# FFN of a hybrid encoder block: first weight sum by an accumulating DMA, 64 pairs by seven for 50, transposes' banks emptied by ScalarE

## The chip, the cores and the metric

The kernel runs on one core of a Trainium2 chip. The time is device microseconds of one execution. A core has TensorE (PE), VectorE (DVE), ScalarE (ACT), GpSimd (POOL) and SyncE (SP), each with its own in-order queue; here SP's queue issues nearly all DMAs and POOL's issues none.

## The reference

One layer of an encoder block on x of 256 tokens x 2048 channels, float32: a norm, a projection, a Hyena branch and a gated-MLP branch, their gated merge and an output projection, and then the part that matters here, a dense SwiGLU FFN with 5632 hidden channels:

```python
h = _rmsnorm(x, norm_ffn_g[l])
gate, up = jnp.split(jnp.einsum('bsd,df->bsf', h, w_ffn_in[l]), 2, axis=-1)
x = x + jnp.einsum('bsf,fd->bsd', jax.nn.silu(gate) * up, w_ffn_out[l])
...
return _rmsnorm(x, norm_final_g)
```

## The kernel before

**Precision by splits.** Every float32 operand of a matmul is split into a high and a low half of type fp32r: ACT casts the high half, DVE subtracts to get the low one (`split_to`, L66). A block product is three matmuls of 512 columns (high x high, high x low, low x high), accumulated in a PSUM bank.

**Weights.** All weights come through one list, `net.halves`. An entry is a 128 x 1024 piece of a weight, which `feed` loads into a "raw" buffer by a DMA on SP's queue and splits, or a function that does something of its own. `take(i)` makes sure that all entries up to i and five more (in the FFN) have been put into the engines' queues. There are six raw buffers and six pairs of high and low buffers.

**The FFN.** The hidden channels go in two parts. Part 0 has 6 chunks of 512 gate and 512 up channels, part 1 has 5. A chunk is one `Quad` over 8 pairs of input blocks: two 128-row blocks of the weight, two column groups of 512 (gate and up), two token tiles of 128. After a part's chunks, two output quads multiply the hidden values H by 12 pairs (part 0) or 10 (part 1) of the output weight. A plain pair has 2 x 2 x 2 = 8 block products (`plain`). A pair "by seven" (`seven`) has 7, by a scheme of Strassen's kind: P1 to P7 and Q4, Q5 use sums of the pair's weights and sums of the activations. P1, Q5, P7 and P6 take the four "aux" banks; P2, N3, Q4 and E, to which plain pairs add, take the other four. `PLAN_IN` and `PLAN_OUT` say which pairs go by seven: three per chunk, and 5, 5, 4 and 3 in the output quads, 50 in all.

**Weight sums.** A pair by seven needs four weights r1 to r4. `quads` makes them as list entries: `one` loads r1 (512 KB), the right half of r4 and the left half of r3 (256 KB each) and lets DVE add r2 = r1 + r4's right half on both halves (128 x 1024, L114), then splits r1; `two` adds r3's right half (512 wide, L119) and splits r2; `three` adds r4's left half (512 wide, L123) and splits r3; the last entry splits r4.

**Activation sums.** When a chunk's last bank is done, DVE combines (`sums`, `finish`), ACT applies silu and DVE multiplies by `up` (L581, two instructions per chunk: this document calls them the multiplications that end a chunk). Four ticks later, that is, after the next chunk's first two pairs, `turn` transposes the result into two aux banks, and the sink `to_h` reads each bank: for a pair that goes by seven in the output quads ACT copies it to the tile "xf" (L590), ACT casts it to H, DVE subtracts H's low half from the bank (L69), and `forms` makes four sums with four 128-wide DVE instructions (L371 to L374) and splits them to HE. Then the second bank's sink follows in the same order. The next quad's P1, Q5, P7 and P6 need aux banks too. `to_x2` does the same for the FFN's input X2, ACT and DVE both reading the bank.

Of the kernel before, what the change touches and what calls it, by code (L numbers as in the profile page):

```python
# [9 lines left out]
F32 = mybir.dt.float32  # L10
F32R = mybir.dt.float32r
# [27 lines left out]
class Net:  # L39
    def __init__(self, nc, tc, a):  # L40
        self.nc, self.tc, self.a = nc, tc, a
        self.halves = []
        self.parts = {}
        self.split_at = 0
        self.ws2 = None
        self.todo = []
        self.raws = self.pairs_ = -1


# [50 lines left out]

    def quads(self, src, seven):


        nc, first, r = self.nc, len(self.halves), {}
        if not seven:
            return self.line(src, 2)

        def one():
            for n in (1, 4, 3, 2):
                r[n] = self.raw_tile()  # L110
            nc.sync.dma_start(out=r[1], in_=src[0])
            nc.sync.dma_start(out=r[4][:, 512:1024], in_=src[1][:, 512:1024])
            nc.sync.dma_start(out=r[3][:, 0:512], in_=src[1][:, 0:512])
            nc.vector.tensor_tensor(out=r[2].rearrange("p (c n) -> p c n", c=2), in0=r[1].rearrange("p (c n) -> p c n", c=2),  # L114
                                    in1=r[4][:, 512:1024].unsqueeze(1).to_broadcast([P, 2, 512]), op=ALU.add)
            return self.split(r[1], 1024)

        def two():
            nc.vector.tensor_tensor(out=r[3][:, 512:1024], in0=r[2][:, 0:512], in1=r[1][:, 512:1024], op=ALU.add)  # L119
            return self.split(r[2], 1024)  # L120

        def three():
            nc.vector.tensor_tensor(out=r[4][:, 0:512], in0=r[3][:, 0:512], in1=r[3][:, 512:1024], op=ALU.add)  # L123
            return self.split(r[3], 1024)
        for fn in (one, two, three, lambda: self.split(r[4], 512)):
            self.halves.append((fn, None, None))
        return first

# [131 lines left out]
class Quad:  # L260
# [31 lines left out]
    def form(self, slot, n):  # L292
        return self.extra[:, slot, 0, n, :], self.extra[:, slot, 1, n, :]

# [5 lines left out]
    def seven(self, at, j, slot):  # L300
        net = self.net
        w = net.take(at)
        self.mul("P1", w, 0, self.at(2 * j, 0))
        self.mul("N3", w, 512, self.form(slot, 1))
        w = net.take(at + 1)
        self.mul("Q5", w, 0, self.form(slot, 2))
        self.mul("P7", w, 512, self.form(slot, 0))
        net.tick()
        w = net.take(at + 2)
        self.mul("P2", w, 0, self.at(2 * j + 1, 0))  # L310
        self.mul("P6", w, 512, self.form(slot, 3))
        w = net.take(at + 3)
        self.mul("Q4", w, 0, self.at(2 * j + 1, 1))
        net.tick()

    def sums(self):

        nc, b = self.net.nc, self.bank
        t = self.t = self.fx.tile([P, 3, 512], F32, name="T")
        d = self.d = self.fx.tile([P, 2, 512], F32, name="D")  # L320
        nc.scalar.copy(out=t[:, 1, :], in_=b["P1"])
        nc.vector.tensor_tensor(out=t[:, 0, :], in0=b["P6"], in1=t[:, 1, :], op=ALU.add)
        nc.vector.tensor_tensor(out=t[:, 2, :], in0=b["P7"], in1=t[:, 0, :], op=ALU.add)
        nc.vector.tensor_tensor(out=d, in0=b["Q5"].unsqueeze(1).to_broadcast([P, 2, 512]), in1=t[:, 0:3:2, :], op=ALU.subtract)
# [35 lines left out]

def forms_tile(fx):

    x = fx.tile([P, 7, P], F32, name="xf")
    return x, (x[:, 0:4:3, :], x[:, 1:3, :])


def forms(net, x, extra, slot):

    nc = net.nc
    x11, x12, x22, x21 = (x[:, n, :] for n in range(4))  # L370
    nc.vector.tensor_tensor(out=x[:, 5, :], in0=x21, in1=x22, op=ALU.subtract)  # L371
    nc.vector.tensor_tensor(out=x[:, 6, :], in0=x[:, 5, :], in1=x11, op=ALU.subtract)
    nc.vector.tensor_tensor(out=x[:, 4, :], in0=x[:, 6, :], in1=x12, op=ALU.add)
    nc.vector.tensor_tensor(out=x21, in0=x11, in1=x21, op=ALU.subtract)  # L374
    net.split_to(extra[:, slot, 0], extra[:, slot, 1], x[:, 3:7, :])

# [15 lines left out]
def build(nc, tc, a):  # L392
# [28 lines left out]
    wo_first = [net.line(a["wout"][n], 8) for n in range(4)]  # L421
    def quads(src, pl):
        return [net.quads(src[j], slot is not None) for j, slot in pl]
    fi_first, fo_first = [], []
    for part in range(2):
        for c in range(CHUNKS[part]):
            fi_first.append(quads(a["wfi"][c + 6 * part], PLAN_IN))
        for n in range(2):
            fo_first.append(quads(a[f"wfo{part}"][n], PLAN_OUT[part][n]))

    with ExitStack() as top:
# [9 lines left out]
        const.tile([P, 40], F32, name="const_pad")  # L441
        ones = net.ones = const.tile([P, P], F32, name="ones")
        nc.vector.memset(ones, 1.0)
        ident = net.ident = const.tile([P, P], F32, name="ident")
# [48 lines left out]
        for n in range(4):  # L493
# [17 lines left out]
        for n in range(4):  # L511
# [4 lines left out]
            if n == 0:  # L516
# [3 lines left out]
                fx = sd.enter_context(tc.tile_pool(name="fx", bufs=1))  # L520
                x2s = ExitStack()
                x2pool = x2s.enter_context(tc.tile_pool(name="x2pool", bufs=1))
                X2 = x2pool.tile([P, KD, 512], F32R, name="X2")
                XE = x2pool.tile([P, 3, 2, 4, P], F32R, name="XE")
            else:
# [7 lines left out]

            def to_x2(n, c):
# [30 lines left out]
        for part in range(2):  # L565
            H = HE = None
            for c in range(CHUNKS[part]):
# [3 lines left out]
                if c == 0:  # L571
# [626 lines left out]
```

## Time and profile before

| | |
|---|---|
| median of three runs | 1366.54 us (1366.52 to 1371.71) |
| the profiled execution's own time | 1369.54 us |
| its span, first to last instruction | 1367.7 us |
| PE / DVE / ACT / POOL busy | 98% / 84% / 57% / 0% |
| mean granted clock of TensorE | 0.997 |
| DMA, mean over the span | 205 GB/s, 280.24 MB |

Busy shares are of the span. The FFN begins near 640 us and takes the rest. A matmul's duration in the trace includes its latency, and matmuls overlap, so the time from one start to the next is the one to count with.

### The profile page before, as it was taken

Reading aid. Unit: us, or ns where it says so; the run is one execution under the profiler, and the core shown is the slowest. Engines: PE = TensorE matmul, PEld = TensorE weight load, DVE = VectorE, ACT = ScalarE, POOL = GpSimd, SP = SyncE. Lnnn points to the kernel's source line nnn. Section 1 sums busy time; section 2 is a strip of 40 time slices with the busy share of each in tenths; the row PEclk is TensorE's granted clock in tenths of the full one; section 3 lists DMA queues with packets and bytes.
Section 4 is the critical chain, followed back from the end, with each engine's and each line's share of the span. In section 5 each row is a group of like instructions: output and inputs, shape, how many; then the busy total and the mean of one; then the engine's idle time right before and its main releaser. Section 6 shows DMA issues by size and latency. Waiting matters only on the chain.

```text
span 1367.7 us, 17785 instructions
## 1 busy us (share of the span) xinstructions
PE 1345.1 (98%) x6404; PEld 1124.0 (82%) x6404; DVE 1143.5 (84%) x1552; ACT 777.4 (57%) x1002; POOL 0.7 (0%) x6
## 2 busy tenths in 40 slices
PE   9999999999999999999999999999999999999996
PEld 7888888888888888888888877878888788878885
DVE  7887789798888766556898989989888889989996
ACT  7665555455545444455666665655555566666653
POOL 0000000000000000000000000000000000000000
PEclk9999999999999999999999999999999999999999
DMA  8775656556555696675556566566766566558853
GB/s 288 254 239 177 193 170 202 168 177 208 164 183 154 233 337 219 183 240 179 197 170 199 200 200 209 163 197 188 243 207 224 185 201 215 172 179 296 281 182 120
DMA packets 89961, 280.24 MB, mean 205 GB/s; under 512 B 9993, under 2 KB 10897, under 8 KB 89233
## 3 DMA queue, kind: packets, MB, share of 16 engines
q1 hardware_dynamic: 87424, 274.84, 61.9%
q10 hardware_dynamic: 2448, 4.27, 0.8%
q8 instruction: 50, 0.82, 0.2%
q14 instruction: 39, 0.31, 0.1%
HBM read 268.58 MB, written 10.49 MB: 204 GB/s over the span
## 4 chain that ended last, share of the span: by engine, by line
PE 83%; DVE 10%; DMA 4%; issue 3%; ACT 1%; DVEq 0%; SPq 0%; ACTq 0%
PE mm L283 16%; PE mg L283 13%; PE mm L138 9%; PE aux L283 8%; PE mg L172 6%; PE mg L174 6%; PE mg L173 6%; PE mm L140 4%; DVE wlo L69 4%; PE mm L174 2%; PE mm L173 2%; PE mm L172 2%; DMA raw<-in_wfi 2%; PE aux L787 2%; DVE raw L114 1%
## 5 line engine op out<-in xcount | busy, mean ns | idle before, releaser
L68 ACT CAST whi<-raw 128x1024 fp32r<-128x1024 f32 (+1 forms) x575 | 572.2, 1010 | 480.8 <-PE mm L283 84.5
L69 DVE TENSOR_TENSOR wlo<-raw,whi 128x1024 fp32r<-128x1024 f32 (+1 forms) x575 | 662.0, 1170 | 165.9 <-ACT whi L68 161.3
L283 PE MATMUL mm<-whi,X 128*128 128x512 f32 x506 | 179.5, 390 | 0.0
L283 PE MATMUL mg<-whi,X 128*128 128x512 f32 x506 | 174.0, 390 | 0.2 <-ACT ne L351 0.2
L138 PE MATMUL mm<-X,whi 128*128 128x512 f32 x512 | 161.4, 396 | 0.0
L140 PEld LDWEIGHTS mm<-X,wlo 128*128 128x128 f32 x512 | 96.1, 188 | 22.6
L283 PEld LDWEIGHTS mg<-whi,X 128*128 128x128 f32 x506 | 95.1, 188 | 20.7 <-ACT ne L351 0.7
L283 PEld LDWEIGHTS mm<-whi,X 128*128 128x128 f32 x506 | 95.3, 188 | 19.9
L140 PE MATMUL mm<-X,wlo 128*128 128x256 f32 x512 | 101.0, 278 | 0.0
L172 PE MATMUL mg<-whi,X 128*128 128x512 f32 x256 | 101.0, 394 | 0.0
L173 PE MATMUL mg<-wlo,X 128*128 128x512 f32 x256 | 99.9, 390 | 0.0
L174 PE MATMUL mg<-whi,X 128*128 128x512 f32 x256 | 99.8, 391 | 0.0
L283 PE MATMUL mm<-wlo,X 128*128 128x512 f32 x253 | 98.7, 390 | 0.0
L283 PE MATMUL mg<-wlo,X 128*128 128x512 f32 x253 | 98.5, 389 | 0.0
L283 PE MATMUL mm<-whi,H 128*128 128x512 f32 x250 | 87.9, 389 | 0.0
L283 PE MATMUL mg<-whi,H 128*128 128x512 f32 x250 | 85.4, 390 | 0.5 <-ACT ne L351 0.5
L283 PE MATMUL aux<-whi,XE 128*128 128x512 f32 x198 | 74.8, 398 | 7.0 <-DVE H L69 6.9
L138 PEld LDWEIGHTS mm<-X,whi 128*128 128x128 f32 x512 | 79.0, 189 | 1.1
L114 DVE TENSOR_TENSOR raw<-raw 128x1024 f32<-128x1024 f32 x50 | 61.0, 1221 | 21.8 <-DMA raw<-in_wfi 12.7
L174 PEld LDWEIGHTS mg<-whi,X 128*128 128x128 f32 x256 | 48.1, 188 | 10.2
L283 PEld LDWEIGHTS mm<-wlo,X 128*128 128x128 f32 x253 | 47.6, 188 | 9.9
L283 PEld LDWEIGHTS mg<-whi,H 128*128 128x128 f32 x250 | 46.9, 188 | 10.6 <-ACT ne L351 0.9
(285 smaller groups left out, 2228.0 us busy)
## 6 DMA issues: line engine op xcount, KB each, us to landing
raw<-in_wfi SPq DMA_DIRECT2D x143, 512.0 KB, 4.2
raw<-in_wfo SPq DMA_DIRECT2D x71, 512.0 KB, 4.3
raw<-in_wg SPq DMA_DIRECT2D x64, 512.0 KB, 3.6
raw<-in_win SPq DMA_DIRECT2D x64, 512.0 KB, 3.6
raw<-in_wfi SPq DMA_DIRECT2D x66, 256.0 KB, 3.1
raw<-in_wbr SPq DMA_DIRECT2D x32, 512.0 KB, 5.5
raw<-in_wout SPq DMA_DIRECT2D x32, 512.0 KB, 3.7
raw<-in_wfo SPq DMA_DIRECT2D x34, 256.0 KB, 3.4
```

Of the source, the lines that this page charges most:

```text
L68: self.nc.scalar.copy(out=hi, in_=src)
L69: self.nc.vector.tensor_tensor(out=lo, in0=src, in1=hi.bitcast(F32), op=ALU.subtract)
L114: nc.vector.tensor_tensor(out=r[2].rearrange("p (c n) -> p c n", c=2), in0=r[1].rearrange("p (c n) -> p c n", c=2), in1=r[4][:, 512:1024]. ...
L138: nc.tensor.matmul(ps[:, 0:512], lhsT=hi[:, col:col + P], rhs=mov, start=start, stop=False)
L140: nc.tensor.matmul(ps[:, 0:256], lhsT=lo[:, col:col + P], rhs=mov[:, 0:256], start=False, stop=stop)
L172: self.nc.tensor.matmul(ps[tt], lhsT=xh, rhs=wh, start=start, stop=False)
L173: self.nc.tensor.matmul(ps[tt], lhsT=xh, rhs=wl, start=False, stop=False)
L174: self.nc.tensor.matmul(ps[tt], lhsT=xl, rhs=wh, start=False, stop=stop)
L283: self.net.nc.tensor.matmul(ps, lhsT=l, rhs=r, start=(n == 0), stop=(n == self.total[name] - 1))
L787: nc.tensor.matmul(ps[:, ri, :], lhsT=fw[:, m + ri, :], rhs=z, start=(n == 0), stop=(n == 2))
```

## The change

Three things are changed, with some moves of memory to make room.

1. r2 is made by DMA. A new list entry, `early`, stands in front of the pair before: SP loads the pair's first piece into a new tile "racc" (two buffers, 512 KB), and POOL issues a DMA that adds the right half of the second piece, read twice from DRAM, onto both halves of it (`accum_op=ALU.add`). `one` then loads r1 (the first piece once more) and r3's left half, without r4's right half; `two` takes "racc" as r2.
2. `PLAN_IN` has four pairs by seven per chunk (2, 3, 5, 6) for three (2, 4, 6); the last two output quads have five each for four and three, the last of them in another order of pairs.
3. In `to_h` ACT copies the bank to SBUF (into "pq", whose content has been transposed) and casts the high half from there; DVE's low half and `forms` follow three or four ticks later. `to_x2` likewise has ACT copy the bank with the scale, and splits from SBUF. `forms` stores three of its sums in the extra tile and the fourth in the place of a block that pairs by seven do not use.

The tile "t5" has four buffers for six, "D" is part of "T", and "ones" lies in another pool.

```diff
+    def quads(self, src, pl):
+        nc, firsts = self.nc, []
+        def early(src):
+            def fn():
+                r2 = self.racc = self.rpool.tile([P, 1024], F32, name="racc", bufs=2)
+                nc.sync.dma_start(out=r2, in_=src[0])
+                nc.gpsimd.dma_start(out=r2.rearrange("p (c n) -> p c n", c=2),
+                                    in_=src[1][:, 512:1024].unsqueeze(1).to_broadcast([P, 2, 512]), accum_op=ALU.add)
+                self.raccs.append(r2)
+            return fn
+        def pieces(src):
+            r = {}
+            def one():
+                for n in (1, 4, 3):
+                    r[n] = self.raw_tile()
+                nc.sync.dma_start(out=r[1], in_=src[0])
+                nc.sync.dma_start(out=r[3][:, 0:512], in_=src[1][:, 0:512])
+                return self.split(r[1], 1024)
+            def two():
+                r[2] = self.raccs.pop(0)
+                nc.vector.tensor_tensor(out=r[3][:, 512:1024], in0=r[2][:, 0:512], in1=r[1][:, 512:1024], op=ALU.add)
+                return self.split(r[2], 1024)
+            def three():
+                nc.vector.tensor_tensor(out=r[4][:, 0:512], in0=r[3][:, 0:512], in1=r[3][:, 512:1024], op=ALU.add)
+                return self.split(r[3], 1024)
+            return one, two, three, lambda: self.split(r[4], 512)
+        for n, (j, slot) in enumerate(pl):
+            if n + 1 < len(pl) and pl[n + 1][1] is not None:
+                self.halves.append((early(src[pl[n + 1][0]]), None, None))
+            firsts.append(len(self.halves))
+            if slot is None:
+                self.line(src[j], 2)
+            else:
+                for fn in pieces(src[j]):
+                    self.halves.append((fn, None, None))
+        return firsts
...
     def form(self, slot, n):
-        return self.extra[:, slot, 0, n, :], self.extra[:, slot, 1, n, :]
+        m = (1, 3, 0, 2)[n]
+        if m == 3:
+            return self.at(2 * slot[1], 1)
+        return self.extra[:, slot[0], 0, m, :], self.extra[:, slot[0], 1, m, :]
...
-        t = self.t = self.fx.tile([P, 3, 512], F32, name="T")
-        d = self.d = self.fx.tile([P, 2, 512], F32, name="D")
+        t = self.t = self.fx.tile([P, 4, 512], F32, name="T")
+        d = self.d = t[:, 0:4:3, :]
...
+def forms(net, fx, x, extra, slot, mov, j):
 
     nc = net.nc
-    x11, x12, x22, x21 = (x[:, n, :] for n in range(4))
-    nc.vector.tensor_tensor(out=x[:, 5, :], in0=x21, in1=x22, op=ALU.subtract)
-    nc.vector.tensor_tensor(out=x[:, 6, :], in0=x[:, 5, :], in1=x11, op=ALU.subtract)
-    nc.vector.tensor_tensor(out=x[:, 4, :], in0=x[:, 6, :], in1=x12, op=ALU.add)
-    nc.vector.tensor_tensor(out=x21, in0=x11, in1=x21, op=ALU.subtract)
-    net.split_to(extra[:, slot, 0], extra[:, slot, 1], x[:, 3:7, :])
+    f = fx.tile([P, 4, P], F32, name="xf")
+    x11, x21, x12, x22 = (x[:, b, P * t:P * (t + 1)] for b in range(2) for t in range(2))
+    nc.vector.tensor_tensor(out=f[:, 0, :], in0=x21, in1=x22, op=ALU.subtract)
+    nc.vector.tensor_tensor(out=f[:, 1, :], in0=x11, in1=x21, op=ALU.subtract)
+    nc.vector.tensor_tensor(out=f[:, 2, :], in0=f[:, 0, :], in1=x11, op=ALU.subtract)
+    nc.vector.tensor_tensor(out=f[:, 3, :], in0=f[:, 2, :], in1=x12, op=ALU.add)
+    net.split_to(extra[:, slot, 0], extra[:, slot, 1], f[:, 0:3, :])
+    net.split_to(mov[:, 2 * j, P:L], mov[:, 2 * j, L + P:2 * L], f[:, 3, :])
...
-PLAN_IN = plan(range(8), (2, 4, 6))
-PLAN_OUT = [[plan(range(12), (2, 4, 6, 8, 10))] * 2, [plan(range(10), (2, 4, 6, 8)), plan(range(10), (2, 4, 6))]]
+PLAN_IN = plan(range(8), (2, 3, 5, 6))
+PLAN_OUT = [[plan(range(12), (2, 4, 6, 8, 10))] * 2,
+            [plan(p, (2, 4, 5, 7, 8)) for p in (range(10), (0, 2, 1, 4, 5, 3, 7, 8, 6, 9))]]
...
-                    t = mpool.tile([P, 512], F32, name="t5", bufs=6)
+                    t = mpool.tile([P, 512], F32, name="t5", bufs=4)
...
+            def to_x2(n, c, xn=xn):
                 def sink(pt):
                     slot = dict(PLAN_IN)[2 * n + c]
+                    flat = xn[:, c, :].rearrange("p (b t) -> p b t", b=2)
+                    j = 4 * n + 2 * c
+                    for b in range(2):
+                        nc.scalar.activation(out=flat[:, b, :], in_=pt[:, b, :], func=AF.Identity,
+                                             scale=par[:, PC_GFFN + j + b:PC_GFFN + j + b + 1])
+                    net.split_to(X2[:, j:j + 2, 0:L], X2[:, j:j + 2, L:2 * L], flat)
                     if slot is not None:
-                        x, halves = forms_tile(fx)
-                        for b in range(2):
-                            j = 4 * n + 2 * c + b
-                            nc.scalar.activation(out=halves[b], in_=pt[:, b, :].rearrange("p (t i) -> p t i", t=2),
-                                                 func=AF.Identity, scale=par[:, PC_GFFN + j:PC_GFFN + j + 1])
-                    for b in range(2):
-                        j = 4 * n + 2 * c + b
-                        gcol = par[:, PC_GFFN + j:PC_GFFN + j + 1]
-                        nc.scalar.activation(out=X2[:, j, 0:L], in_=pt[:, b, :], func=AF.Identity, scale=gcol)
-                        nc.vector.scalar_tensor_tensor(out=X2[:, j, L:2 * L], in0=pt[:, b, :], scalar=gcol,
-                                                       in1=X2[:, j, 0:L].bitcast(F32), op0=ALU.mult, op1=ALU.subtract)
-                    if slot is not None:
-                        forms(net, x, XE, slot)
+                        forms(net, fx, flat, XE, slot, X2, 2 * n + c)
...
-                def to_h(j, H=H, HE=HE, slots=dict(PLAN_OUT[part][0])):
+                def to_h(j, pq=pq, H=H, HE=HE, slots=dict(PLAN_OUT[part][0])):
                     def sink(pt):
                         slot = slots[j]
-                        if slot is not None:
-                            x, halves = forms_tile(fx)
-                            for b in range(2):
-                                nc.scalar.copy(out=halves[b], in_=pt[:, b, :].rearrange("p (t i) -> p t i", t=2))
-                        net.split_to(H[:, 2 * j:2 * j + 2, 0:L], H[:, 2 * j:2 * j + 2, L:2 * L], pt)
-                        if slot is not None:
-                            forms(net, x, HE, slot)
+                        flat = pq[:, j % 2, :].rearrange("p (b t) -> p b t", b=2)
+                        nc.scalar.copy(out=flat, in_=pt)
+                        hi, lo = H[:, 2 * j:2 * j + 2, 0:L], H[:, 2 * j:2 * j + 2, L:2 * L]
+                        nc.scalar.copy(out=hi, in_=flat)
+                        def rest():
+                            nc.vector.tensor_tensor(out=lo, in0=flat, in1=hi.bitcast(F32), op=ALU.subtract)
+                            if slot is not None:
+                                forms(net, fx, flat, HE, slot, H, j)
+                        net.later(3 + j % 2, rest)
```

The lines of the old `quads` and `forms` that go are in the listing above.

## Rows read from the trace of the kernel before

**Rows 1.** The page: span, busy time of each engine, the large DMA queue.

```profile
span 1367.7 us, 17785 instructions
...
PE 1345.1 (98%) x6404; PEld 1124.0 (82%) x6404; DVE 1143.5 (84%) x1552; ACT 777.4 (57%) x1002; POOL 0.7 (0%) x6
...
q1 hardware_dynamic: 87424, 274.84, 61.9%
```

**Rows 2.** Windows: length; PE, PEld, DVE, ACT, POOL busy (instructions); granted clock; DMA share; GB/s.

```profile
783.30:827.50 44.20, 43.05 (x195) 35.25 (x194) 39.70 (x46) 26.84 (x34) 0.00 (x0) 1.00 0.57 190
827.50:871.70 44.20, 42.64 (x192) 35.10 (x191) 41.29 (x48) 27.17 (x34) 0.00 (x0) 1.00 0.62 202
1080.00:1100.00 20.00, 17.75 (x76) 14.26 (x75) 18.03 (x21) 10.51 (x14) 0.00 (x0) 0.91 0.48 147
1240.00:1260.00 20.00, 20.00 (x90) 16.57 (x89) 18.27 (x20) 12.63 (x17) 0.00 (x0) 1.00 0.79 289
1260.00:1280.00 20.00, 20.00 (x93) 16.36 (x92) 20.00 (x23) 11.32 (x15) 0.00 (x0) 1.00 0.86 322
```

**Rows 3.** Waits of TensorE, 700 to 1300 us: total, times, longest.

```profile
PE aux L283 <- DVE H L69: 8.4, 5, 2.3
```

**Rows 4.** Timeline of a bank wait: start, length (us), engine, line, operation, count.

```profile
826.19 0.33 SPq L111 DMA_DIRECT2D raw<-in_wfi  x1
...
830.45 1.03 PE L203 MATMUL aux<-ident,pq 128*128 128x128 f32 x8
...
831.24 0.48 PE L283 MATMUL aux<-whi,X 128*128 128x512 f32 x1
...
831.71 0.64 ACT L590 COPY xf<-aux 128x256 f32<-128x256 f32 x2
...
832.03 1.22 DVE L114 TENSOR_TENSOR raw<-raw 128x1024 f32<-128x1024 f32 x1
...
835.03 0.68 DVE L69 TENSOR_TENSOR H<-aux,H 128x512 fp32r<-128x512 f32 x1
835.63 0.28 DVE L371 TENSOR_TENSOR xf<-xf 128x128 f32<-128x128 f32 x1
...
835.77 0.50 PE L283 MATMUL aux<-whi,XE 128*128 128x512 f32 x1 [1.56 <-DVE H L69]
835.83 0.69 DVE L69 TENSOR_TENSOR H<-aux,H 128x512 fp32r<-128x512 f32 x1
...
837.03 2.35 DVE L69 TENSOR_TENSOR wlo<-raw,whi 128x1024 fp32r<-128x1024 f32 x2
```

**Rows 5.** Chain that ended last: start, length, what.

```profile
727.20 2.04 PE mg L283 x9
```

**Rows 6.** Groups by shape, 700 to 1300 us: count, busy, mean ns, idle before.

```profile
L114 DVE TENSOR_TENSOR raw<-raw 128x1024 f32<-128x1024 f32 x43 | 52.5, 1221 | 18.9 <-DMA raw<-in_wfi 9.8 <-DMA raw<-in_wfo 9.1
...
L68 ACT CAST whi<-raw 128x512 fp32r<-128x512 f32 x43 | 26.7, 620 | 35.0 <-DVE raw L123 35.0
...
L68 ACT CAST H<-aux 128x512 fp32r<-128x512 f32 x22 | 11.9, 600 | 0.0
```

**Rows 7.** Timeline of VectorE: the multiplications that end a chunk.

```profile
696.52 1.42 DVE L581 SCALAR_TENSOR_TENSOR pq<-ne,r,pq 128x512 f32<-128x512 f32 x2
...
826.04 1.41 DVE L581 SCALAR_TENSOR_TENSOR pq<-ne,r,pq 128x512 f32<-128x512 f32 x2
...
913.92 1.42 DVE L581 SCALAR_TENSOR_TENSOR pq<-ne,r,pq 128x512 f32<-128x512 f32 x2
```

**Rows 8.** DMA issues: KB each, median us to landing; landings of tile raw.

```profile
raw<-in_wfi SPq DMA_DIRECT2D x143, 512.0 KB, 4.2
yacc<-y_d SPq DMA_DIRECT2D x2, 1024.0 KB, 10.8
other<-p_d SPq DMA_DIRECT2D x2, 1024.0 KB, 8.9
DMA to landing us min/median/max: 2.6/3.9/8.1
```

More of the change, by code (lines that the diff above doesn't have):

```diff
@@ L47, in __init__ @@
         self.raws = self.pairs_ = -1
+        self.raccs = []
     def chunk(self, pieces, cuts=1):
@@ L99, in feed @@
             self.split_at += 1
[L101 to L127, printed above, removed]
@@ L303, in seven @@
         self.mul("P1", w, 0, self.at(2 * j, 0))
-        self.mul("N3", w, 512, self.form(slot, 1))
+        self.mul("N3", w, 512, self.form((slot, j), 1))
         w = net.take(at + 1)
-        self.mul("Q5", w, 0, self.form(slot, 2))
-        self.mul("P7", w, 512, self.form(slot, 0))
+        self.mul("Q5", w, 0, self.form((slot, j), 2))
+        self.mul("P7", w, 512, self.form((slot, j), 0))
         net.tick()
@@ L310, in seven @@
         self.mul("P2", w, 0, self.at(2 * j + 1, 0))
-        self.mul("P6", w, 512, self.form(slot, 3))
+        self.mul("P6", w, 512, self.form((slot, j), 3))
         w = net.take(at + 3)
@@ L358, in finish @@
         nc.vector.tensor_tensor(out=ne, in0=ne, in1=self.d, op=ALU.add)
[L361 to L367, printed above, removed]
+def forms(net, fx, x, extra, slot, mov, j):
     nc = net.nc
-    x11, x12, x22, x21 = (x[:, n, :] for n in range(4))
-    nc.vector.tensor_tensor(out=x[:, 5, :], in0=x21, in1=x22, op=ALU.subtract)
-    nc.vector.tensor_tensor(out=x[:, 6, :], in0=x[:, 5, :], in1=x11, op=ALU.subtract)
-    nc.vector.tensor_tensor(out=x[:, 4, :], in0=x[:, 6, :], in1=x12, op=ALU.add)
-    nc.vector.tensor_tensor(out=x21, in0=x11, in1=x21, op=ALU.subtract)
-    net.split_to(extra[:, slot, 0], extra[:, slot, 1], x[:, 3:7, :])
+    f = fx.tile([P, 4, P], F32, name="xf")
[6 more added lines that the diff above has]
+    net.split_to(mov[:, 2 * j, P:L], mov[:, 2 * j, L + P:2 * L], f[:, 3, :])
 def plan(pairs, seven):
     return [(j, seven.index(j) if j in seven else None) for j in pairs]
-PLAN_IN = plan(range(8), (2, 4, 6))
-PLAN_OUT = [[plan(range(12), (2, 4, 6, 8, 10))] * 2, [plan(range(10), (2, 4, 6, 8)), plan(range(10), (2, 4, 6))]]
+PLAN_IN = plan(range(8), (2, 3, 5, 6))
+PLAN_OUT = [[plan(range(12), (2, 4, 6, 8, 10))] * 2,
+            [plan(p, (2, 4, 5, 7, 8)) for p in (range(10), (0, 2, 1, 4, 5, 3, 7, 8, 6, 9))]]
 CHUNKS = (6, 5)
@@ L421, in build @@
     wo_first = [net.line(a["wout"][n], 8) for n in range(4)]
-    def quads(src, pl):
-        return [net.quads(src[j], slot is not None) for j, slot in pl]
     fi_first, fo_first = [], []
@@ L426, in build @@
         for c in range(CHUNKS[part]):
-            fi_first.append(quads(a["wfi"][c + 6 * part], PLAN_IN))
+            fi_first.append(net.quads(a["wfi"][c + 6 * part], PLAN_IN))
         for n in range(2):
-            fo_first.append(quads(a[f"wfo{part}"][n], PLAN_OUT[part][n]))
+            fo_first.append(net.quads(a[f"wfo{part}"][n], PLAN_OUT[part][n]))
     with ExitStack() as top:
@@ L441, in build @@
         const.tile([P, 40], F32, name="const_pad")
-        ones = net.ones = const.tile([P, P], F32, name="ones")
-        nc.vector.memset(ones, 1.0)
         ident = net.ident = const.tile([P, P], F32, name="ident")
@@ L453, in build @@
         ev = left.enter_context(tc.tile_pool(name="ev", bufs=1))
+        ones = net.ones = ev.tile([P, P], F32, name="ones")
+        nc.vector.memset(ones, 1.0)
         ys_pool = left.enter_context(tc.tile_pool(name="ys_pool", bufs=1))
@@ L521, in build @@
                 x2s = ExitStack()
+                net.rpool = sd.enter_context(tc.tile_pool(name="rpool", bufs=1))
                 x2pool = x2s.enter_context(tc.tile_pool(name="x2pool", bufs=1))
                 X2 = x2pool.tile([P, KD, 512], F32R, name="X2")
-                XE = x2pool.tile([P, 3, 2, 4, P], F32R, name="XE")
+                XE = x2pool.tile([P, 4, 2, 3, P], F32R, name="XE")
             else:
@@ L532, in build @@
                 nc.scalar.activation(out=sq[:, 0, :], in_=y, func=AF.Square, accum_out=ss[:, 0, tt, n:n + 1])
-            def to_x2(n, c):
+            xn = fx.tile([P, 2, 512], F32, name="ne")
+            def to_x2(n, c, xn=xn):
                 def sink(pt):
                     slot = dict(PLAN_IN)[2 * n + c]
-                    if slot is not None:
-                        x, halves = forms_tile(fx)
-                        for b in range(2):
-                            j = 4 * n + 2 * c + b
-                            nc.scalar.activation(out=halves[b], in_=pt[:, b, :].rearrange("p (t i) -> p t i", t=2),
-                                                 func=AF.Identity, scale=par[:, PC_GFFN + j:PC_GFFN + j + 1])
-                    for b in range(2):
-                        j = 4 * n + 2 * c + b
-                        gcol = par[:, PC_GFFN + j:PC_GFFN + j + 1]
-                        nc.scalar.activation(out=X2[:, j, 0:L], in_=pt[:, b, :], func=AF.Identity, scale=gcol)
-                        nc.vector.scalar_tensor_tensor(out=X2[:, j, L:2 * L], in0=pt[:, b, :], scalar=gcol,
-                                                       in1=X2[:, j, 0:L].bitcast(F32), op0=ALU.mult, op1=ALU.subtract)
-                    if slot is not None:
-                        forms(net, x, XE, slot)
+                    flat = xn[:, c, :].rearrange("p (b t) -> p b t", b=2)
[4 more added lines that the diff above has]
+                    net.split_to(X2[:, j:j + 2, 0:L], X2[:, j:j + 2, L:2 * L], flat)
+                    if slot is not None:
+                        forms(net, fx, flat, XE, slot, X2, 2 * n + c)
                 return sink
@@ L576, in build @@
                     H = hpool.tile([P, 24, 512], F32R, name="H")
-                    HE = hpool.tile([P, 5, 2, 4, P], F32R, name="HE")
+                    HE = hpool.tile([P, 5, 2, 3, P], F32R, name="HE")
                 q.finish(pq, ne)
```

## The prediction

> **What bounds the kernel now.** I read the page's busy shares first. TensorE (PE) is busy for 1345.1 of 1367.7 us, VectorE (DVE) for 84%, ScalarE (ACT) for 57%, POOL for 0.7 us in all; the one large DMA queue fills 61.9% of the engines' time [rows 1]. So at most 22.6 us can come from filling PE's gaps, and anything beyond that must take matmuls away. Next, windows over the FFN, since all that the change touches lies behind 600 us. In two windows of 44.2 us, about one chunk each, PE is idle 1.2 and 1.6 us, DVE busy 39.7 and 41.3 us, the DMA engines 57 and 62% [rows 2]. PE bounds, with DVE close behind. The table of PE's waits between 700 and 1300 us names one cause: 8.4 us, in five waits, for DVE's low half of H [rows 3]. The timeline of one of them shows how [rows 4]. Eight transposes run at 830.45; ACT copies the `forms` operands out of the first bank at 831.71, but DVE has a weight sum and two more instructions ahead of its own read of that bank and reaches it at 835.03, and the second bank at 835.83. PE, which needs these banks for P7 and P6 of the first pair by seven, sits idle 1.56 us before 835.77. Around one such wait the granted clock is 0.91 over 20 us [rows 2], so 1.8 us go there beside the wait.
>
> **Matmuls removed.** A plain pair is 8 block products of 3 matmuls, a pair by seven 7 of 3. In the chain of waits nine matmuls in a row take 2.04 us [rows 5]: 0.227 us each. (The 0.48 and 0.50 us of single ones in [rows 4] are latency, not pitch.) Fourteen more pairs by seven (one in each of 11 chunks, three in the last two output quads) remove 14 x 3 x 0.227 = 9.5 us. They lie where PE is the bound, so all of it counts.
>
> **The banks' emptying.** After the change ACT alone reads them: copy, high half, copy, high half, some 0.6 us each by the H cast of [rows 6], 2.4 us for both banks, the low halves and `forms` coming three or four ticks later from SBUF. P7 follows the transposes by 9 matmuls, 2.0 us, and P6 by 2.7 or more; the first bank is free after 0.6 us, the second after 1.8. What can hold ACT is the cast of the pair's fourth weight, queued in front, which needs DVE's two short sums. Placed on the times of that chunk: the multiplications at a chunk's end run from 826.04 to 827.45 [rows 7]; DVE then needs 1.13 + 0.60 + 1.13 + 0.60 us up to that sum, to 830.9; the cast ends at 831.5, after the transposes (831.24), and the banks are free at 832.1 and 833.3. P7 wants its bank at 831.24 + 2.04 = 833.3, P6 at 834.0: it fits, by about a microsecond. So the 8.4 us and the 1.8 us of clock go: 10.2 us. A check: multiplications lie (913.92 - 696.52) / 5 = 43.5 us apart [rows 7], while 183 matmuls x 0.227 and 0.8 us of transposes [rows 4] make 42.3 us: 1.2 us are lost per chunk, about ten times.
>
> **DVE.** Two 1024-wide instructions in a row take 2.35 us, so 1.13 each, a 512-wide one is followed after 0.60 us, a 128-wide one after 0.20 [rows 4]. A chunk before: 5 plain pairs x 2 x 1.13 = 11.3; 3 by seven x (4 x 1.13 + 3 x 0.60) = 19.0; sums, `finish` and multiplications 0.6 + 0.6 + 3 x 1.13 + 1.4 = 6.0; H 2 x 0.6 and, for nine chunks in ten, `forms` 4 x 0.2 + 0.6: 2.5. Together 38.8 us. After: 4 x 2.26 = 9.0; 4 x (3 x 1.13 + 3 x 0.60) = 20.8; 6.0; 2.6: 38.4 us, against 180 x 0.227 + 0.8 = 41.6 us on PE. The first sum, 50 x 1.22 us (L114, of which [rows 6] has 43), more than pays for the added pairs. DVE stays under PE with 3 us to spare per chunk, and its 18.9 us of waits for DMA before L114 [rows 6] go. ACT gets 1.5 casts more per added pair and a copy per bank, some 2.5 us on the 27 of [rows 2]; DVE is the later of the two in any case, so this is hidden unless ACT blocks. Dropping "t5" to four buffers and moving "ones" costs nothing: a fourth-back "t5" has been read by its add or transposes several ticks earlier.
>
> **The accumulating DMA.** Its chain per pair: SP's issue, 0.33 us; the load of "racc", 512 KB, median 4.2 us [rows 8]; POOL's issue; the accumulation; then DVE's second sum and ACT's cast. No row shows the last DMA. POOL's issue lies between SP's 0.33 us [rows 4] and 5.5 us, the spread of landings between 2.6 and 8.1 [rows 8]; I take 0.33. The accumulation brings 512 KB and has to read the 512 KB that are there: it is nearest to the 1024 KB rows, 8.9 and 10.8 us [rows 8]; below, a fast plain load, 2.6; above, two slow ones, 16.2. I take 8.9. Sum 13.8 us, ends 5.9 and 30 (0.33 + 2.6 + 0.33 + 2.6; 0.33 + 8.1 + 5.5 + 16.2).
>
> The time it has: two "racc" buffers, so the load for pair 5 waits for pair 2's second split, that for 6 for pair 3's. From there to the second sum of 5 DVE does, with 1.73 for a short sum and a long split, 1.73 + 0.6 (rest of 2), 1.13 + 1.73 + 1.73 + 0.6 (pair 3), 2.26 (pair 4), 2.6 (H, `forms`) and 1.13 (first split of 5) = 13.5 us, paced by PE some 14.6; the second sum itself may come about 2 us late before PE starves, since splits run several halves ahead. So up to 16.5 us nothing is lost. In the output quads a pair by seven follows a plain one, or the buffer is free earlier, and 14.5 to 17 us are there. SP's queue is held while it waits for "racc", with the r1 and r3 loads of the next pair behind; r1 of pair 5 then lands some 6 us after pair 3's second split, and DVE wants it after 7.
>
> Bandwidth: a chunk moved 8 x 1.05 = 8.4 MB (190 and 202 GB/s [rows 2]). After, a pair by seven moves 0.52 + 0.52 + 0.26 + 0.52 = 1.83 MB, 2.36 with the read of the tile: 11.5 to 13.6 MB in 41.6 us, 277 to 328 GB/s. The stretch at 322 GB/s had the engines at 0.86 [rows 2], which makes 374 the ceiling. It fits, but not everywhere: between 1240 and 1280 us, where `yacc` and `other` come in, (289 + 322) x 20 us = 12.2 MB move [rows 2]; four pairs by seven there add 3.1 to 5.2 MB, against 15.0 MB of room: 0.3 to 2.4 MB too much, 1 to 6 us, of which I take 3. For the thinner cover elsewhere I take 0.25 us for each of ten chunks, 2.5.
>
> **Sum.** The profiled execution took 1369.54 us, 1.84 more than its span and 3.0 above the median of the runs. 1369.5 - 9.5 - 10.2 + 5.5 = 1355.3; less 3.0, 1352.
>
> **Rivals.**
>
> *A, the waits stay.* ACT stands behind a cast that waits for DVE's sums, and P7 waits as before. For it: ACT's short casts waited 35.0 us for L123 [rows 6]. Against: the sum in front of them is gone. Then only the matmuls count: 1357 without, 1363 with the new waits.
>
> *B, the accumulation comes late (the other side).* DVE's second sum in pair 5 stops, everything queued behind it on DVE and ACT too, and PE starves for T - 16.5 us per chunk. At T = 18 that is 11 x 1.5 = 16 us, 1369, no gain; at T = 20, 38 us and some 10 in the output quads, 1400. For it: the range of T; a chain of two transfers at 62% load and rising. Against: the row of 1024 KB. It turns slower from T near 18.5. An accumulation at a quarter of a load's rate would also fill the engines: 17.8 MB a chunk at 374 GB/s are 47.6 us.
>
> *C, POOL and DVE get in each other's way.* If making descriptors held DVE for one long instruction, 1.22 us [rows 6], four times per chunk, 4.9 us would stand against 3.2 of room: 1.7 x 11 = 19 us, 1371. From 0.8 us a time PE feels it. Against: POOL has nothing else to do; no row shows the two together.
> The Trainium skill (SBUF — State Buffer, Who interferes with whom) bears on C: GpSimd shares its SBUF ports with VectorE, and a VectorE instruction with two SBUF inputs, as nearly all are here, contends with GpSimd's reads, not with its writes. By that rule C needs descriptor making to read SBUF; no run here shows it, and if it only writes, C's time is the forecast's.
>
> **Chances.** Forecast (1345 to 1358) 0.62, A 0.14, B 0.18, C 0.06. This kernel's measurement tells 0.5% from no change, 1360 to 1373. Faster: 0.62 + 0.05 of A = 0.67; same: 0.09 of A, 0.02 of B, 0.01 of C = 0.12; slower: 0.16 of B, 0.05 of C = 0.21. Forecast and A end at 1363; the range reaches into B to T near 19, 1388, which leaves out 0.13 above and a few hundredths below 1345 (all 20 us gained, no new wait, would be 1347).
>
> **What would show it.** Right: PE has 42 matmuls fewer; its waits for H on aux banks are gone; multiplications 41.6 to 42.3 us apart; L123's place on DVE waits little for DMA; accumulations land within 9 us. Wrong: DVE idle before the second sum, released by the accumulation, longest in pairs 5 and 6; aux banks waiting for ACT's copies (A); DVE instructions longer than 1.22 us beside POOL's (C); DMA share above 0.95.

## The result, and the profile after

The changed kernel takes 1420.01 us (median of 4 runs, 1418.14 to 1424.31) beside 1366.91 us for the kernel before on the same chip: a ratio of 1.0384, 95% interval 1.0356 to 1.0413. It is slower by 53 us, 68 us above the forecast and 32 above the range.

The page of the kernel after: span, busy times, the two queues that matter (q1 is fed by SP, q0 by POOL), and some DMA issues (KB each, median us to landing). They answer to [rows 1] and [rows 8].

```profile
span 1416.3 us, 17989 instructions
...
PE 1356.8 (96%) x6362; PEld 1125.9 (79%) x6362; DVE 1130.9 (80%) x1574; ACT 806.4 (57%) x1052; POOL 77.9 (6%) x70
...
q1 hardware_dynamic: 89440, 291.62, 61.2%
q0 software_dynamic: 17408, 33.56, 14.2%
...
raw<-in_wfi SPq DMA_DIRECT2D x132, 512.0 KB, 6.1
...
racc<-in_wfi SPq DMA_DIRECT2D x44, 512.0 KB, 5.5
racc<-in_wfi POOLq DMA_DIRECT2D x44, 512.0 KB, 7.7
```

The change did what it says: 42 matmuls fewer, 64 accumulations, DVE's busy time down. But raw loads that landed after 4.2 us [rows 8] now take 6.1. The same 600 us of the FFN, first in the kernel before and then in the kernel after (columns as in [rows 2]):

```profile
700.00:1300.00 600.00, 590.67 (x2630) 485.81 (x2629) 538.43 (x590) 363.81 (x441) 0.00 (x0) 1.00 0.63 208
```

```profile
700.00:1300.00 600.00, 566.19 (x2459) 462.54 (x2458) 494.10 (x570) 362.04 (x449) 60.17 (x50) 0.97 0.87 259
```

PE gets through 171 matmuls fewer in the same time. At 590.67 / 2630 = 0.2246 us each that is 38 us: 24.5 are added idle time (600 - 566.2 against 600 - 590.7), and 14 are slower matmuls, 566.19 / 2459 = 0.2303 us, with the granted clock at 0.97. Some 4 us more had been lost before (the first chunk ends 3.6 us later, with a pair by seven more), and the rest is lost past 1300 us, where the last output quads run. The chunks are (926.00 - 700.14) / 5 = 45.2 us apart by the multiplications that end them, not the 41.6 to 42.3 of the forecast and not the 43.5 of [rows 7]:

```profile
700.14 1.41 DVE L596 SCALAR_TENSOR_TENSOR pq<-ne,r,pq 128x512 f32<-128x512 f32 x2
...
926.00 1.41 DVE L596 SCALAR_TENSOR_TENSOR pq<-ne,r,pq 128x512 f32<-128x512 f32 x2
```

The waits of PE in these 600 us, beside [rows 3], and then groups by shape (count, busy, mean ns, idle before and its releasers), beside [rows 6]:

```profile
PE mg L302 <- ACT ne L373: 21.1, 9, 3.2
PE mg L302 <- DVE wlo L70: 8.0, 3, 3.5
PE mg L302 <- ACT pq L373: 3.0, 2, 1.6
PE aux L302 <- DVE wlo L70: 1.5, 2, 0.9
```

```profile
L69 ACT CAST whi<-raw 128x1024 fp32r<-128x1024 f32 x210 | 218.2, 1052 | 140.2 <-DMA raw<-in_wfi 51.6 <-PE mm L302 41.2 <-issue 14.6
...
L112 POOL DMA_DIRECT2D racc<-in_wfi x38 | 45.7, 1203 | 399.3 <-DMA racc<-in_wfi 179.7 <-DVE raw L133 83.9 <-DVE wlo L70 38.7
...
L129 DVE TENSOR_TENSOR raw<-racc,raw 128x512 f32<-128x512 f32 x50 | 34.4, 687 | 46.9 <-issue 12.3 <-DMA racc<-in_wfo 9.5 <-DMA raw<-in_wfi 9.1
```

The waits for H are gone. In their place PE waits for L373: ACT's copies of a finished quad's banks, which the next quad adds to. These copies are not slow (0.6 us); ACT comes late to them, because it stands at casts of weights whose loads have not landed, 51.6 us in all. The chain of waits shows one (start, length, what):

```profile
774.41 8.88 DMA raw<-in_wfi
783.29 0.02 issue
783.31 0.04 ACTq L69
783.35 0.04 issue
783.39 0.16 ACT whi L69
783.54 0.79 issue
784.34 0.59 ACT ne L373
784.93 0.04 issue
784.97 2.83 PE mg L302 x6
```

A load issued at 774.41 takes 8.88 us. ACT's cast waits for it, the copy of the bank is queued behind the cast, and PE stands 2.10 us for the bank:

```profile
784.97 0.69 PE L302 MATMUL mg<-whi,X 128*128 128x512 f32 x1 [2.10 <-ACT ne L373]
```

The windows of the same stretch say why the load took so long:

```profile
776.00:778.00 2.00, 2.00 (x11) 1.65 (x10) 2.00 (x3) 0.48 (x1) 0.00 (x0) 1.00 1.05 335
778.00:780.00 2.00, 2.00 (x11) 1.65 (x10) 0.61 (x2) 1.05 (x1) 0.00 (x0) 1.00 1.04 383
780.00:782.00 2.00, 2.00 (x10) 1.68 (x9) 1.72 (x3) 1.05 (x1) 0.00 (x0) 1.00 1.02 415
```

The DMA engines were full. Over the whole stretch the share is 0.87, but it is made of such bursts.

Not every wait starts at a plain load. The waits for "wlo" go back, all but 0.65 us, to accumulations that landed late, as this part of the chain shows:

```profile
1001.04 10.00 DMA racc<-in_wfo
...
1011.12 0.70 DVE raw L129
...
1012.45 1.23 DVE wlo L70
```

This accumulation takes 10.00 us; DVE's second sum (L129) waits for it, and PE waits for the split behind. With every wait followed back in this way to the first DMA, 24.8 of PE's 33.6 us of waits start at plain loads, and 8.8 at accumulations. Of the 24.8 us, 23.5 belong to loads that SP had issued within 0.4 us of their buffer coming free: they were not sent late, they landed late.

### The profile page after: what moved, and what is told of

It reads as the page before. It is cut to its first block, busy times and chain, and to the rows that moved or that the text cites. A ratio compares the mean times of both kernels' runs of the same rounds, so it can differ in the third digit from the quotient of the medians.

```text
span 1416.3 us, 17989 instructions
## 1 busy us (share of the span) xinstructions
PE 1356.8 (96%) x6362; PEld 1125.9 (79%) x6362; DVE 1130.9 (80%) x1574; ACT 806.4 (57%) x1052; POOL 77.9 (6%) x70
## 3 DMA queue, kind: packets, MB, share of 16 engines
q0 software_dynamic: 17408, 33.56, 14.2%
## 4 chain that ended last, share of the span: by engine, by line
PE 63%; DMA 19%; DVE 10%; issue 4%; ACT 2%; SPq 1%; DVEq 0%; ACTq 0%; POOLq 0%
PE mm L157 8%; PE mm L302 8%; DMA raw<-in_wfi 8%; PE mg L302 7%; PE mg L191 6%; PE mg L192 6%; PE mg L193 6%; DVE wlo L70 6%; DMA racc<-in_wfi 4%; PE mm L159 4%; PE aux L302 4%; DMA racc<-in_wfo 4%; PE mm L193 2%; PE mm L192 2%; PE mm L191 2%
## 5 line engine op out<-in xcount | busy, mean ns | idle before, releaser
L69 ACT CAST whi<-raw 128x1024 fp32r<-128x1024 f32 (+1 forms) x539 | 528.1, 995 | 448.9 <-PE mg L193 77.3
L70 DVE TENSOR_TENSOR wlo<-raw,whi 128x1024 fp32r<-128x1024 f32 (+1 forms) x539 | 609.1, 1151 | 168.0 <-ACT whi L69 161.7
L302 PE MATMUL mm<-whi,X 128*128 128x512 f32 x528 | 195.3, 397 | 0.1
L302 PE MATMUL mg<-whi,X 128*128 128x512 f32 x440 | 159.1, 402 | 21.6 <-ACT ne L373 18.5
L302 PEld LDWEIGHTS mg<-whi,X 128*128 128x128 f32 x440 | 85.2, 194 | 44.4 <-ACT ne L373 22.4
L112 POOL DMA_DIRECT2D racc<-in_wfi x44 | 53.1, 1218 | 1079.6 <-DMA racc<-in_wfi 839.7
L69 ACT CAST whi<-racc 128x1024 fp32r<-128x1024 f32 x64 | 67.5, 1055 | 60.2 <-PE mm L302 20.5
L191 PE MATMUL mg<-whi,X 128*128 128x512 f32 x256 | 101.0, 394 | 0.0
L193 PE MATMUL mg<-whi,X 128*128 128x512 f32 x256 | 99.8, 390 | 0.0
L302 PE MATMUL aux<-whi,XE 128*128 128x512 f32 x264 | 95.6, 389 | 0.0
L129 DVE TENSOR_TENSOR raw<-racc,raw 128x512 f32<-128x512 f32 x64 | 44.0, 687 | 60.7 <-DMA racc<-in_wfo 15.7
L70 DVE TENSOR_TENSOR wlo<-racc,whi 128x1024 fp32r<-128x1024 f32 x64 | 78.1, 1220 | 11.9 <-ACT whi L69 11.7
```

Of the source, the lines that this page charges most:

```text
L69: self.nc.scalar.copy(out=hi, in_=src)
L70: self.nc.vector.tensor_tensor(out=lo, in0=src, in1=hi.bitcast(F32), op=ALU.subtract)
L112: nc.gpsimd.dma_start(out=r2.rearrange("p (c n) -> p c n", c=2), in_=src[1][:, 512:1024].unsqueeze(1).to_broadcast([P, 2, 512]), accum_op= ...
L191: self.nc.tensor.matmul(ps[tt], lhsT=xh, rhs=wh, start=start, stop=False)
L193: self.nc.tensor.matmul(ps[tt], lhsT=xl, rhs=wh, start=False, stop=stop)
L302: self.net.nc.tensor.matmul(ps, lhsT=l, rhs=r, start=(n == 0), stop=(n == self.total[name] - 1))
```

## The experiments

Theories: **V**, the DMA engines are full, so that the kernel's own loads land late; **L**, the chain of load, accumulation and second sum is too long (rival B); **H**, SP is held at the load of "racc", with other loads queued behind. Each ratio is against the kernel before, run on the same chip (its medians 1369.25, 1368.51 and 1369.16 us in the three groups). In e1, e3, e7 and e11, whose two last output quads differ in their pairs by seven, the last quad's plain pair 8 multiplies a block that `forms` has replaced by a sum; the work done is the same.

**e3: the emptying alone.** The changed kernel with DVE making the first sum as before, and with the old 50 pairs.

```diff
+                nc.sync.dma_start(out=r[4][:, 512:1024], in_=src[1][:, 512:1024])
+                nc.vector.tensor_tensor(out=r[2]..., in0=r[1]..., in1=r[4][:, 512:1024]..., op=ALU.add)
-                r[2] = self.raccs.pop(0)
-                self.halves.append((early(src[pl[n + 1][0]]), None, None))
-PLAN_IN = plan(range(8), (2, 3, 5, 6))
+PLAN_IN = plan(range(8), (2, 4, 6))
```

> ScalarE's emptying of the transposes' banks alone: first sum by VectorE, 50 pairs as before. V, H and L: the waits for H (8.4 us) and the clock's 1.8 us go, 1354 to 1359 us. Rival: ScalarE's copies stand behind casts that wait for weights, and the waits return under another name, 1364 to 1368 us.

Measured 1359.33 us, ratio 0.9935 (0.9912 to 0.9958), 0.3 us above the expected range: a gain of 9.9 us, where the prediction's step had 10.2. The windows show PE without a gap:

```profile
700.00:1300.00 600.00, 599.90 (x2688) 496.53 (x2688) 550.05 (x611) 377.80 (x462) 0.00 (x0) 1.00 0.63 211
```

**e2: 64 pairs with DVE's sums.** As e3, but with the plans of the change.

> The changed kernel with VectorE making the first sum as before (no accumulating DMA, no racc), 64 pairs by seven and ScalarE's emptying kept. V, H and L alike: the 36 us of PE waits that DMAs end go, and VectorE has 42.9 us of work in a chunk against 41.6 us of TensorE, so 1365 to 1375 us. If the 64 pairs or their places (2, 3, 5, 6) were the cause, and not the accumulating DMA: 1400 us or more.

Measured 1373.01, ratio 1.0030 (1.0013 to 1.0047), inside the range: the 64 pairs and their places are not the cause. DVE is busy for 578.1 of those 600 us: the pairs added don't pay as long as it makes the sums.

**e1: the accumulating DMA with 50 pairs.** The changed kernel with the old plans.

> The changed kernel with the plans of before: 50 pairs by seven (2, 4, 6 per chunk), the accumulating DMA and ScalarE's emptying kept. Theory V (volume: the accumulations and the second load of the first piece fill the DMA engines in bursts, plain loads land late): DMA bytes of 50 accumulations for 64, so the loss shrinks but stays, 1385 to 1400 us. Theory H (hold: SP's queue stands while it waits for one of two racc buffers, and the loads behind it go out late): in alternating pairs the buffer is free long before, so the loss goes, 1357 to 1370 us. Theory L (chain: the accumulation itself ends after VectorE wants it): alternating pairs leave 14.5 us and more for 14.7, so 1365 to 1380 us.

Measured 1384.56, ratio 1.0115 (1.0094 to 1.0136), 0.4 us below V's range and 4.6 above L's. Beside e3 the sum by DMA costs 25.2 us, though it takes work off DVE.

```profile
700.00:1300.00 600.00, 582.19 (x2574) 477.38 (x2573) 476.70 (x543) 357.64 (x444) 50.37 (x42) 0.99 0.84 257
```

The chain shows that these 25.2 us are not V's alone (one of four such places):

```profile
739.57 1.15 DVE wlo L70
...
740.73 0.33 SPq L111
...
741.48 4.40 DMA raw<-in_wfi
```

This raw load's buffer had been free since 727.16, but it was issued at 741.48, because SP stood 5.3 of these 14.3 us at the load of "racc" in front (L111) until DVE's split freed its buffer. Of PE's 18.1 us of waits past 640 us, 6.4 start at such held loads (H), 7.1 at late accumulations (L), 3.4 at plain loads that were issued at once and landed late (V); 1.2 can't be followed to a DMA.

**e4: the changed kernel with DVE reading the banks again** (`lo` from `pt`, without `later`).

> The changed kernel (accumulating DMA, 64 pairs) with VectorE reading H's low half from the bank at once, as before, not ScalarE alone. If the emptying by ScalarE is worth what the prediction said, 10 us, this is 1425 to 1432 us. If ScalarE's added copies (0.6 us each, in front of casts) are part of the loss, it is 1400 to 1415 us.

Measured 1423.1, ratio 1.0402 (1.0376 to 1.0429), which can't be told from the changed kernel's. Its waits for H hardly return: 0.4 us in 700 to 1300 us, and one of 4.8 us later, which goes back to the load of "other". The expectation held neither way, and no run shows why the emptying is worth so little here.

**e6: the load of "racc" on POOL's queue.**

```diff
-                nc.sync.dma_start(out=r2, in_=src[0])
+                nc.gpsimd.dma_start(out=r2, in_=src[0])
```

> The changed kernel with racc's load issued on POOL's queue, so that SP's queue never stands for racc. H: 1360 to 1380 us. V: the same bytes, 1410 to 1430 us. L: the load starts no earlier and POOL's issue of 1.2 us comes twice, 1415 to 1435 us.

Measured 1440.05, ratio 1.0536 (1.0504 to 1.0568): 20 us worse than the change and above all three ranges. SP no longer waits for "racc", and nothing is gained, so H falls as the cause of the change's loss, as the issue times above say too. Why it is worse is not settled: of its 59.9 us of PE waits past 640 us, 18.8 start at late accumulations, where the change has 12.9 of 44.7. The Trainium skill (DMA: Bandwidth & Descriptors, Issuing engines are not separate DMA queues) says that a DMA runs on the same 16 engines whichever engine issues it, so another issuer saves the time of issue alone. This run agrees: the engines' share in 700 to 1300 us is 0.84 beside 0.87, and no time is won.

**e7: the traffic without a consumer.** e3 with the DMAs of `early` added, into tiles that nothing reads.

> The kernel of e3 (VectorE makes the first sum, 50 pairs) with the two DMAs of the entry early put back but their result read by nobody: all the traffic of e1 and r4's right half on top, no chain that VectorE waits for, and racc free as soon as the DMAs are done. V: as slow as e1 or nearly, 1378 to 1395 us. H and L: as e3, 1358 to 1363 us.

Measured 1480.6, ratio 1.0812 (1.0794 to 1.0830), above either range. Only the two "racc" buffers paced these DMAs, and all 50 accumulations ran between 540 and 925 us. The windows of e7 during and after:

```profile
660.00:900.00 240.00, 161.57 (x617) 126.66 (x616) 128.08 (x160) 93.77 (x123) 40.94 (x34) 0.82 0.99 277
900.00:1080.00 180.00, 180.00 (x805) 149.22 (x805) 165.11 (x192) 114.65 (x142) 1.20 (x1) 0.99 0.61 195
```

With the engines full PE stands for a third of the time; once the DMAs are through, for none. Full engines moved only 277 GB/s here. But e7 doesn't tell V from H. With nobody reading "racc", a buffer is free only when its accumulation has landed, and SP stood for that, with the kernel's own loads behind (SP's waits between 540 and 925 us):

```profile
SPq L111 <- DMA racc<-in_wfi: 174.4, 41, 10.7
SPq L111 <- DMA racc<-in_wfo: 75.0, 18, 8.5
```

That is 249 of 385 us. Of PE's 84.3 us of waits between 640 and 930 us, 49.4 start at loads that were issued 1.8 to 8.4 us after their buffers had come free.

**e5: a quarter of the accumulation.** The changed kernel, accumulating onto 128 of each 512 columns; the other columns of r2 stay unsummed.

```diff
-                nc.gpsimd.dma_start(out=r2.rearrange("p (c n) -> p c n", c=2), ...
+                nc.gpsimd.dma_start(out=r2.rearrange("p (c n) -> p c n", c=2)[:, :, 0:128], ...
```

> The changed kernel with the accumulation cut to 128 of the 512 columns on each half (the rest of r2 is left as loaded; order, waits and the number of DMAs stay). V: three quarters of the accumulations' engine time go (64 x 2.4 us of the 16 engines), so most of the loss goes: 1360 to 1375 us. H: the racc buffers are freed by the same VectorE instructions, so 1405 us or more. L: the chain is some 4 us shorter, 1365 to 1390 us.

Measured 1365.19, ratio 0.9976 (0.9963 to 0.9990), inside V's range and L's: 55 us come back, but this run doesn't choose.

**e12: a plain write for the accumulation.** The same 512 KB on the same queue, without `accum_op`.

> The changed kernel with the second DMA of a sum a plain write in place of an accumulation, of the same 512 KB on the same queue: r2 then holds the second block and not the sum of two. Its packets should take about 84 ns for 2 KB, not 178, so a chunk's DMA work falls from about 41 to about 35 us of PE's 41.6. V (the DMA engines are full): 1375 to 1395, share in 700 to 1300 us at 0.72 to 0.78, raw loads back under 5.5 us. L (the chain's length or its waits set the loss, whatever the engines carry): the chain is only some 3 us shorter, 1400 to 1415.

Measured 1373.86, ratio 1.0033 (1.0020 to 1.0046): 46 us come back. The queue and the window of e12:

```profile
q0 software_dynamic: 9216, 33.56, 7.7%
```

```profile
700.00:1300.00 600.00, 583.32 (x2580) 477.50 (x2579) 520.38 (x603) 382.75 (x475) 39.02 (x54) 0.99 0.79 275
```

The same 33.56 MB take 7.7% of the engines' time where accumulation takes 14.2%, and more GB/s pass (275 against 259) at a lower share (0.79 against 0.87). So it is the time of the packets that fills the engines, not the bytes. The result is just under V's range and far under L's; the share is 0.01 above what V expected. The write is also sooner done (5.7 us against 7.7, and POOL's issue 0.72 against 1.20), and raw loads still took 5.6 us, not under 5.5; so the chain is a little shorter too, and by itself e12 would not exclude a stronger form of L.

**e11: the unused traffic, paced.** e7 with a one-column DVE copy that ties each "racc" to the split before it.

```diff
+                nc.vector.tensor_copy(out=r2[:, 0:1], in_=self.lastlo.bitcast(F32)[:, 0:1])
```

> The kernel with ScalarE emptying the banks, VectorE's sums and 50 pairs, with the loads and the accumulating DMAs of the change issued as well, into a tile that nothing reads; a tiny VectorE copy into its first column, from the split before, spaces them along the chunks (in the run before, without it, they were all issued early). The last output quad's plain pair 8 multiplies a block that a sum has replaced, so the output is not the reference's. V (the DMA engines are full, so the kernel's own loads land late): the DMAs cost by their traffic alone, 1378 to 1400, as the run with 50 pairs and the accumulation in use (1384.6), with the share of the DMA engines at 0.80 or more in 700 to 1300 us and raw loads landing later than 5 us. L (the chain of load and accumulation ends late and VectorE waits for it): nobody waits for it here, so 1358 to 1363, as the run without these DMAs (1359.3).

Measured 1431.02, ratio 1.0451 (1.0434 to 1.0467): 72 us over e3 with nobody waiting for the chain's end (no wait of DVE is for "racc"). The share in 700 to 1300 us is 0.84 and raw loads land after 5.4 us, as V expected. The waits of PE in e11, 700 to 1300 us:

```profile
PE mg L306 <- ACT ne L377: 24.5, 9, 3.7
PE mg L306 <- DVE wlo L70: 13.4, 6, 5.1
```

It is the signature of the changed kernel: ACT late at the banks behind loads that land late. L is not needed for it. Of PE's 48.7 us of waits past 640 us, 30.7 start at loads that were issued as their buffer came free and took 4.9 to 9.5 us (e3's raw loads take 3.6 in the median); 7.9 start at one load that SP held back, and 10.2 can't be followed to a DMA. The size is above V's range, which was set by e1; but e11 moves 13.1 MB more than e1 (301.06 against 287.95 MB on q1, the right halves of r4 still being loaded) and has 50 copies that hold SP's queue (47.7 us of waits in 700 to 1300 us), so 72 us is not the price of the accumulation alone.

**e8 and e9: what is worth keeping.** e3's emptying and sums, the pairs by seven put elsewhere: in e8 three per chunk and five in every output quad, 53; in e9 three in the last two, 49.

```diff
+PLAN_OUT = [[plan(range(12), (2, 4, 6, 8, 10))] * 2, [plan(range(10), (2, 4, 6))] * 2]
```

> No accumulating DMA: first sum by VectorE, ScalarE's emptying, three pairs by seven per chunk as before, five in each output quad (53 in all). VectorE has room in the output quads (54 us of work for 62 of TensorE), so the three added pairs give their 2 us: 1355 to 1359 us, under e3 and both kernels of the change. If any added pair costs VectorE time that TensorE then waits for: 1360 us or more.

> The change's emptying of the transposes' banks by ScalarE alone, kept by itself: no accumulating DMA, VectorE makes every first sum, and the pairs by seven are taken off the last output quads, where VectorE was busy throughout in the run with 53 of them: three in each chunk's inner quads, five and five in the output quads but the last two, three and three there, 49 in all. Each pair moved costs 3 matmuls of 0.227 us, and the profile of the run with 50 pairs and VectorE's sums showed 1359.3. If VectorE is what ends last in those quads: 1355 to 1360, at or a little under that run. If it isn't: one pair fewer is 0.7 us slower, 1360 to 1361. Valid output.

e8 measured 1365.29, ratio 0.9971 (0.9957 to 0.9985), a miss of the 1355 to 1359: in the last output quads DVE is busy for 29.9 of 30 us (1300 to 1330) and PE for 27.5. e9 measured 1359.13, ratio 0.9928 (0.9916 to 0.9939). It beats both kernels, by 0.7% and, by 0.9928 / 1.0384, 4.4%, and no accumulating DMA is in it. It can't be told from e3, so whether DVE still ends last in those quads stays open.

## Why the prediction was wrong

**The step that failed is the bandwidth.** The prediction took 374 GB/s as "the ceiling", from one stretch at 322 GB/s and 0.86, counted 277 to 328 GB/s for a chunk, and said "it fits"; its new waits, a term of 5.5 us, measured some 70. Three things are wrong in it.

First, the ceiling. The chunk windows in [rows 2], the ones to which the load is added, give 190 / 0.57 = 333 and 202 / 0.62 = 326 GB/s; the best stretch was taken in their place. The whole run says the same: 0.619 x 1367.7 us / 274.84 MB [rows 1] is 3.08 us of all engines per MB, 325 GB/s.

Second, the currency. What runs out is the engines' time, and a MB has no fixed price: the 2 us windows in the first section pass 335 to 415 GB/s at a full share. By the q0 rows an accumulated MB takes 0.142 x 1416.3 / 33.56 = 5.99 us, a plain one on the same queue 0.077 x 1374.5 / 33.56 = 3.15: 1.90 times as much. (The Trainium skill, Collectives: The Full Stack, The bandwidth ceiling: the fold count and why AG ≠ RS ≠ AR, has reduce at half the rate of copy in the collectives' ring, since an add needs two source reads. This ratio is near that; that reads are the reason no run here shows.) The upper end of 2.36 MB, which counted the tile's read, was the right one. A chunk then needs, as an estimate, 9.4 MB x 3.08 + 2.1 MB x 5.99 = 41.6 us of the DMA engines, and PE wanted its chunk done in 41.6. The five chunks between the multiplications shown above measured 0.87 x 45.2 = 39.3 us:

```profile
700.14:926.00 225.86, 213.31 (x934) 174.55 (x933) 194.29 (x230) 143.67 (x183) 24.06 (x20) 0.98 0.87 258
```

Third, a share below one was costed at almost nothing. The same count for the other runs, as an estimate, with what the five chunks measured (share x spacing), beside what each run lost in all against e3, where a pair more is credited with 0.68 us:

| run | DMA time per chunk / PE's time | measured | lost |
|---|---|---|---|
| e3, DVE's sums, 50 pairs | 25.9 / 42.3 = 61% | 25.3 us | 0 |
| e5, a quarter accumulated, 64 | 33.4 / 41.6 = 80% | 32.0 us | 15 us |
| e12, plain write, 64 | 35.7 / 41.6 = 86% | 33.4 us | 24 us |
| e1, accumulation, 50 | 37.7 / 42.3 = 89% | 35.9 us | 25 us |
| e11, unused accumulation, 50 | 40.2 / 42.3 = 95% | 37.9 us | 72 us |
| the change, 64 | 41.6 / 41.6 = 100% | 39.3 us | 70 us |

The estimates are 2 to 7% high. The shares order the runs, but H and L have parts in the losses (in e1 above all), and no share is a threshold. In e5 the first part's last five chunks run at a share of 0.77 and are 41.6 us apart, PE's own pace; the second part's last four run at 0.76 and are 43.3 apart:

```profile
695.99:904.07 208.08, 207.14 (x935) 171.62 (x934) 193.57 (x230) 144.28 (x183) 24.07 (x20) 1.00 0.77 244
1075.57:1248.73 173.16, 168.66 (x749) 138.23 (x748) 156.66 (x189) 115.93 (x148) 19.25 (x16) 0.99 0.76 239
```

Loads come in bursts: the engines are at 1.0 for 6 us on end, a load takes 8.88 us, and the six raw buffers don't cover that. Even with the prediction's own 13.6 MB and 374 GB/s the share was 88%, near the 89% estimated for e1, which lost 25 us. The prediction's own sign, a share above 0.95, shows in such bursts and not in the mean of 0.87.

**What else the steps had.** *Matmuls removed*: 42, and the pitch of 0.227 us stands in the chain (six in 1.36 us); what they save in all could not be timed, since each run with 64 pairs has another bound somewhere (DVE in e2; late DMAs in e5, e12 and the change). In e5's five chunks above it can: 41.6 us apart for e3's 42.2, 0.57 us for the 0.68 forecast. *The banks' emptying*: right; e3 gives 9.9 us for 10.2, and rival A falls with it. *DVE*: 194.29 / 5 = 38.9 us per chunk for 38.4 worked out. *The accumulating DMA's chain*: by the medians 0.33 + 5.5 + 1.2 + 7.7 = 14.7 us for 13.8; POOL's issue, taken at 0.33, is 1.20, and the accumulation 7.7, not 8.9. That stays under the cover of 16.5, but medians hide the late ones: in 700 to 1300 us a load of "racc" takes up to 12.5 us and an accumulation up to 11.3, and DVE's second sum waits 16.9 us for "racc". So rival B's first mechanism did come, with 8.8 of PE's 33.6 us of waits; it is not what sets most of the loss. B's last sentence, that a slow accumulation would also fill the engines, named the right mechanism at the wrong threshold: half of a load's rate was enough, not a quarter. *Rival C* does not appear: DVE's 128x1024 subtractions take 1.22 us beside 64 issues of POOL, as before.

**What stays open.** A longer lead (more "racc" or raw buffers) wasn't tried. How much of the 70 us is the burst's shape and how much the mean load isn't separated, and the drop of the granted clock was not varied by itself.

## What to carry to other kernels

Moving work from an engine to the DMAs is paid in time of the DMA engines: price each kind of transfer by its queue's share x span / MB in a profile, and an accumulation into SBUF at about twice a plain write. Take the rate at full share from the stretch to which the load is added, not from the best stretch. And plan for well under a full share: here some chunks at 0.77 lost nothing and others at 0.76 lost 1.7 us each, and the loss showed up on an engine that merely had a cast of a late weight queued in front of something PE needed. In an experiment that only adds traffic, look whether the added DMAs hold the queue that issues the others: in e7 they did.

## What the runs showed that was not expected

- The accumulation went out in packets of half the size: q0 counts 17,408 packets for 33.56 MB, and 9,216 for the same bytes written plainly.
- POOL's issue instruction took 1203 ns for an accumulation and 722 ns for the plain write, where SP's takes 0.33 us.
- A quarter of the columns (8.39 MB) still cost 5.1% of the engines, 0.051 x 1365.5 / 8.39 = 8.3 us per MB: the number of packets counts beside the bytes.
